# Recurrent outputs stored as split pairs, and the softmax factors, high parts and gather of an attention stage moved to other engines

## Chip, cores and metric

The kernel runs on one core of one Trainium2 chip. The metric is the device time of one execution in microseconds (us). Engines are called by the profile's short names: PE is TensorE (matmuls), DVE is VectorE, ACT is ScalarE, POOL is GpSimd, SP is SyncE, whose queue issues most of the DMAs.

## What is computed

One decoder block with two branches over a sequence of 2048 tokens and a width of 1024. One wide projection feeds a recurrence (causal convolution, then a gated linear scan) and an attention over three dilated windows. Each branch is multiplied by a gate and projected, the two are merged, projected again and normalised.

```python
proj = h @ w_in[l]
x_rnn, z_rnn, q, k, v, z_attn, g_r, g_a = jnp.split(proj, IN_SPLITS, axis=-1)
xc = causal_depthwise_conv(x_rnn, conv_w[l], conv_b[l])
hr = rg_lru(xc, w_a[l], b_a[l], w_x[l], b_x[l], lam[l], positions)
y_rnn = (hr * jax.nn.silu(z_rnn.astype(jnp.float32))).astype(dt) @ w_out_rnn[l]
...
o = dilated_attention_mixture(qh, kh, vh).reshape(B, S, D_ATTN)
y_attn = (o * jax.nn.silu(z_attn.astype(jnp.float32))).astype(dt) @ w_out_attn[l]
merged = jax.nn.sigmoid(g_r + bg_r) * y_rnn + jax.nn.sigmoid(g_a + bg_a) * y_attn
x = x + gate[:, None, :] * (merged @ w_o[l])
return rms_norm(x, g_final)
```

## The kernel before

**Split operands.** Every fp32 matmul operand is held as a rounded high part (type float32r) and a low part, the difference. A product is three matmuls (`mm3`, L147): high by high, high by low, low by high. `hi_act` (L152) rounds on ACT and `hi_dve` (L155) on DVE; `lo_pool` (L158) subtracts on POOL and `lo_dve` (L161) on DVE. The page books these under L153, L156, L159 and L162.

**First stage.** Two halves of the sequence (f = 0 and 1) run through the input projection by a Strassen scheme (`strassen`, L270; seven products of twelve matmuls each). In between, `recurrent` (L596) runs for eight channel blocks m. Its work on a half has ten steps spread over the products that follow (`steps_after`, L202): taps, gates, exponentials, scan, and at step 10 `finish` (L678), which multiplies the scan by the gate on DVE in the tile `zs` and stores 128x512 fp32 to the scratch tensor `yaT` on SP. The order in this stage comes from a scheduler with its own time model. `zs` has two buffers.

**Attention stage.** From L1361 on, the order is written by hand. 16 heads (8 for each half; the second half has more keys) have six units each: four of kind "c" (one class of token positions, both longer dilations) and two of kind "w" (the local blocks of 128). Time is cut into slots, one unit's scores to a slot. For a unit in slot s: PE makes the scores into PSUM (tag `sc`, two buffers), DVE takes the row minimum (`softmax_tile`, L983) and ACT the exponential with its sum into `st`. Seven slots later PE transposes the tile (`transposes_c`, `transposes_w`), `split_p` (L1057) splits it from PSUM into `pth` (high, ACT) and `ptl` (low, DVE), and a slot after that PE multiplies it by the values.

At the end of the slot ahead of the transposes, `scale` (L1046) multiplies the exponentials by a factor for each row, on DVE for "c" and on ACT for "w". Those factors are made once per head: `gather` (L1136, two POOL instructions, tile `sm`, at the tail of the head's last score slot), `exchange` in the next slot (one matmul into a third `sc` tile, so it needs one of the two buffers back from the row minimum), `maxima` on DVE, `exponentials` on ACT, `weights` on DVE. Within a slot the places are HEAD, scores, SOFTMAX, two thirds of the fill, EXCHANGE, one third of the fill, WEIGHTS, transposes, sums, TAIL.

**The fill.** `steps` (L1267) is a generator of matmul steps of the two output projections, some 3.2 to 3.6 steps (three 128x512 matmuls each) for each slot: four jobs on the recurrent outputs `yaT`, then two on the attention outputs `oT`. A job is 8 output blocks by 8 steps. While a job's last block (m = 7) runs, the operands `Y[j + 1, k]` of the next one are made: `load_y` (L1278) loads to `yraw` (four buffers) on SP, and `split_y` (L1285) makes `yh` on ACT and `yl` on POOL, eight buffers each, so that a buffer comes free when the step that reads it is done. Loads of keys, queries (`kraw`), values (`vraw`), weights (`w`) and gates (`fg`) go through the same SP queue in program order.

After the attention the rest of the fill runs, then the last products and the output projection with the final norm.

Of the kernel before, what the change touches and what calls it, by code (L numbers as in the profile page):

```python
# [20 lines left out]
P = 128  # L21
# [63 lines left out]
def decoder_block(ctx, tc, x, c, positions, g_norm, w_mod, b_mod, w_in, b_gate, conv_w, conv_b,  # L85
# [10 lines left out]
    def scratch(name, shape):  # L96
        return nc.dram_tensor(name, shape, F32, kind="Internal").ap()
# [54 lines left out]
    def hi_act(o, i):  # L152
        nc.scalar.activation(o, i, AF.Copy)  # L153
# [442 lines left out]
    def recurrent(rp, bigr, f, m):  # L596
# [25 lines left out]
        def x_part(j, ps, u):  # L622
# [67 lines left out]
        def done(i, j, ps, u):  # L690
            (z_part if i else x_part)(j, ps, u)
# [224 lines left out]
    def at(slot, place, fn, *args):  # L916
        plan.setdefault((slot, place), []).append((fn, args))
# [5 lines left out]
    class Head:  # L923
# [121 lines left out]

        def scale(self, kind, x):  # L1046
            for i, pp in enumerate(self.u[kind, x]):
                if kind == "c":
                    nc.vector.tensor_scalar(pp, pp, self.M[:, 0, x, i : i + 1], None, ALU.mult)  # L1049
                else:  # L1050
                    pp = pp[0][:, pp[1] :]
                    nc.scalar.activation(pp, pp, AF.Copy, scale=self.M[:, 1, i, x : x + 1])

        def transposes(self, kind, x):
            (self.transposes_c if kind == "c" else self.transposes_w)(x)

        def split_p(self, pt, cols):  # L1057
            th = T(ap_, [P, CH], F32R, "pth", bufs=4)
            tl = T(ap_, [P, CH], F32R, "ptl", bufs=4)
            hi_act(th[:, cols], pt[:, cols])  # L1060
            lo_dve(tl[:, cols], pt[:, cols], th[:, cols])
            return th, tl

        def transposes_c(self, r):
            pp, out = self.u.pop(("c", r)), []
            for k0 in range(0, self.bk[1] + 1, 2):
                pt = T(pT, [P, CH], F32, "pT")
                w = 2 * P + (P if k0 + 1 == self.bk[1] else 2 * P)
                for k in (k0, k0 + 1):
                    c0 = (k % 2) * 2 * P  # L1070
                    for j, i in enumerate([i for i, n in enumerate(self.bk) if n >= k]):
                        nc.tensor.transpose(pt[:, c0 + j * P : c0 + (j + 1) * P], pp[i][:, k * P : (k + 1) * P], ident)
                out.append(self.split_p(pt, slice(0, w)))
            self.u["tc", r] = out

        def transposes_w(self, i):

            pt_, out = self.u.pop(("w", i)), []
            for pieces in ((1, 2, 3, 4), (5, 6, 7, 0)):
                pt = T(pT, [P, CH], F32, "pT")  # L1080
                if self.bk[i] == 0 and 0 in pieces:
                    pieces = pieces[:3]
                for c, x in enumerate(pieces):
                    pp, half = pt_[x // 2][0], x % 2
                    nc.tensor.transpose(pt[:, c * P : (c + 1) * P], pp[:, half * P : (half + 1) * P], ident)
                out.append(self.split_p(pt, slice(0, len(pieces) * P)))
            self.u["tw", i] = out


# [46 lines left out]
        def gather(self):  # L1136

            self.sm = T(ap_, [P, 2, 4, 2, 8], F32, "sm")
            for g in range(2):
                nc.gpsimd.tensor_tensor(  # L1140
                    self.sm[:, g], self.st[:, :, g].rearrange("p t b n -> p t (b n)").unsqueeze(1).broadcast_to([P, 4, 2, 8]),
                    qm.unsqueeze(2).unsqueeze(3).broadcast_to([P, 4, 2, 8]), ALU.mult)

# [54 lines left out]
        def enlist(self, B):  # L1198
# [68 lines left out]
    def steps(jobs):  # L1267
# [8 lines left out]
                W[x] = load_wd(jobs[j][0], m, x % 2)  # L1276

        def load_y(j, k):  # L1278
            if j < len(jobs):
                w, ys, n = jobs[j]  # L1280
                assert ys is yaT or all((n // 2, h, n % 2) in stored for h in range(H))
                t = raw["y", j, k] = T(fl, [P, CH], F32, "yraw", bufs=4)
                nc.sync.dma_start(t[:], ys[k * P : (k + 1) * P, n * CH : (n + 1) * CH])
# [197 lines left out]
```

## Time and profile before

| | us |
|---|---|
| runs shown (median, lowest to highest) | 2396.06 (2392.12 to 2398.46) |
| the profiled execution, its own time | 2398.24 |
| its span, first to last instruction | 2396.5 |
| first attention scores to the last | 1508.7 to 2064.7 |
| loads of `yraw` from `yaT` | 1479.8 to 1754.6 |

In a row of the groups, the number after the bar is the busy time, then the mean of one instruction in ns; after the second bar stands the time for which the engine sat idle just ahead of these instructions and what ended it. In a timeline row the bracket holds the same for one instruction. In a row by stretches, each engine has its busy time and number of instructions; PEclk is the clock that PE was granted, as a share of full speed, and the next number is the busy share of the 16 DMA engines.

### The profile page before, as it was taken

What the parts mean: (1) busy time and instruction counts of PE and PEld (TensorE: products, weight loads), DVE (VectorE), ACT (ScalarE), POOL (GpSimd) and SP (SyncE); (2) the same over time, 40 slices, a digit from 0 to 9 for tenths busy, and PEclk for the clock granted to TensorE, in tenths of its full rate; (3) what the DMA queues carried; (4) which work ended last, traced back from release to release, by engine and by line L of the source; (5) the groups of instructions that cost most, each with busy time, mean ns of one, the idle gap of its engine ahead of it and who ended that gap; (6) DMA issues with size and microseconds to landing.
All of it is one profiled execution on the core that took longest, in us unless ns stands there. A gap on an engine that the chain in (4) does not pass through costs nothing.

```text
span 2396.5 us, 34064 instructions
## 1 busy us (share of the span) xinstructions
PE 2245.3 (94%) x11397; PEld 1884.5 (79%) x11397; DVE 1392.2 (58%) x2439; ACT 1137.7 (47%) x2268; POOL 1034.0 (43%) x813
## 2 busy tenths in 40 slices
PE   5899999999989999999999998999989898989998
PEld 5897777777777897878888876888878787878887
DVE  6847666766585734443444561477767787845433
ACT  3436656666542525555444411565666666522211
POOL 2566556665554643332211011456565757342000
PEclk9999999999999999999999998999999999999999
DMA  7266877677778559999666776988887678698752
GB/s 264 85 216 216 277 252 263 234 265 252 245 261 267 164 165 330 314 325 294 211 222 224 263 230 228 282 244 261 262 255 240 215 226 253 211 316 278 234 189 97
DMA packets 416295, 577.06 MB, mean 241 GB/s; under 512 B 71934, under 2 KB 278006, under 8 KB 415096
## 3 DMA queue, kind: packets, MB, share of 16 engines
q1 hardware_dynamic: 378680, 455.33, 60.7%
q10 hardware_dynamic: 37440, 119.55, 13.1%
q8 instruction: 90, 1.47, 0.2%
q14 instruction: 85, 0.70, 0.1%
HBM read 362.95 MB, written 211.82 MB: 240 GB/s over the span
## 4 chain that ended last, share of the span: by engine, by line
PE 55%; DMA 10%; DVE 10%; issue 9%; POOL 7%; ACT 5%; SPq 3%; ACTq 1%; POOLq 0%; DVEq 0%
PE pj L145 42%; PE pq L145 7%; PE pg L145 2%; PE sc L145 1%; PE o L145 1%; POOL S L159 1%; DMA wraw<-in_w_in_dram 1%; POOL yl L159 1%; DVE acc L485 1%; DMA wD<-s 1%; POOL vh L159 1%; POOL kq L159 1%; DMA yraw<-yaT 1%; DMA fg<-mrT 1%; DMA vraw<-vN 1%
## 5 line engine op out<-in xcount | busy, mean ns | idle before, releaser
L145 PE MATMUL pj<-T,S 128*128 128x512 f32 x4704 | 1121.5, 398 | 28.6 <-DVE ev L338 17.3
L145 PEld LDWEIGHTS pj<-T,S 128*128 128x128 f32 x4704 | 890.4, 190 | 248.0 <-DVE ev L338 22.5
L145 PE MATMUL pj<-yh,w 128*128 128x512 f32 x1024 | 373.8, 410 | 10.7 <-ACT yh L153 10.7
L159 POOL TENSOR_TENSOR S<-wraw,S 128x512 fp32r<-128x512 f32 x168 | 240.0, 1441 | 176.0 <-ACT S L186 105.0
L145 PEld LDWEIGHTS pj<-yh,w 128*128 128x128 f32 x1024 | 197.6, 193 | 47.8 <-ACT yh L153 11.8
L987 ACT ACTIVATE pp<-pp,st 128x256 f32<-128x256 f32 (+3 forms) x256 | 133.5, 523 | 171.0 <-DVE st L986 171.0
L145 PE MATMUL pj<-yl,w 128*128 128x512 f32 x512 | 205.3, 401 | 2.6 <-POOL yl L159 2.5
L145 PE MATMUL pj<-S,T 128*128 128x256 f32 x1152 | 161.1, 295 | 11.3 <-POOL S L159 7.9
L162 DVE TENSOR_TENSOR ptl<-pT,pth 128x384 fp32r<-128x384 f32 (+1 forms) x160 | 94.8, 626 | 124.6 <-ACT pth L153 124.4
L145 PEld LDWEIGHTS pj<-S,T 128*128 128x128 f32 x1152 | 150.8, 200 | 13.7 <-POOL S L159 9.4
L159 POOL TENSOR_TENSOR S<-s,S 128x512 fp32r<-128x512 f32 x84 | 114.4, 1362 | 91.5 <-ACT S L186 55.3
L159 POOL TENSOR_TENSOR yl<-yraw,yh 128x512 fp32r<-128x512 f32 x64 | 84.8, 1350 | 125.7 <-DMA yraw<-yaT 63.5
L640 DVE SCALAR_TENSOR_TENSOR xc<-xr,par,xc 128x512 f32<-128x512 f32 x96 | 83.5, 870 | 60.5 <-ACT xc L634 57.4
L1049 DVE TENSOR_SCALAR pp<-pp,M 128x128 f32<-128x128 f32 (+3 forms) x128 | 117.3, 956 | 0.0
L159 POOL TENSOR_TENSOR wh<-vraw,wh 128x640 fp32r<-128x640 f32 (+1 forms) x32 | 48.3, 1510 | 159.2 <-ACT wh L153 135.9
L292 DVE TENSOR_TENSOR u<-pj,u 128x512 f32<-128x512 f32 x56 | 38.4, 685 | 134.7 <-PE pj L145 79.5
L145 PEld LDWEIGHTS pj<-yl,w 128*128 128x128 f32 x512 | 99.1, 194 | 19.0 <-POOL yl L159 5.8
L986 DVE CUSTOM_DVE_ANT_0 pp<-sc,msk 128x256 f32<-128x256 f32 (+3 forms) x256 | 102.7, 444 | 16.1 <-PE sc L145 15.7
L159 POOL TENSOR_TENSOR kq<-kraw,kq 128x512 fp32r<-128x512 f32 (+1 forms) x64 | 102.1, 1607 | 13.8 <-ACT kq L153 13.8
L145 PE MATMUL pq<-oh,mh 128*128 128x512 f32 x256 | 98.6, 394 | 8.9 <-ACT mh L153 8.9
L620 POOL TENSOR_TENSOR zs<-zs,sg 128x512 f32<-128x512 f32 x32 | 46.0, 1437 | 133.1 <-ACT sg L616 132.5
L145 PE MATMUL pq<-ol,mh 128*128 128x512 f32 x256 | 100.7, 393 | 0.0
(287 smaller groups left out, 3996.1 us busy)
## 6 DMA issues: line engine op xcount, KB each, us to landing
sD<-S ACTq DMA_DIRECT2D x196, 512.0 KB, 3.4
S<-sD SPq DMA_DIRECT2D x196, 512.0 KB, 5.3
w<-wD SPq DMA_DIRECT2D x128, 512.0 KB, 5.7
wraw<-in_w_in_dram SPq DMA_DIRECT2D x136, 256.0 KB, 3.4
wD<-s ACTq DMA_DIRECT2D x64, 256.0 KB, 4.0
T<-in_w_mod_dram SPq DMA_DIRECT2D x8, 1024.0 KB, 9.6
vN<-ev SPq DMA_DIRECT2D x64, 128.0 KB, 2.3
zaT<-ev SPq DMA_DIRECT2D x32, 256.0 KB, 3.4
```

What stands on the lines that cost most here:

```text
L145: last_mm[0] = nc.tensor.matmul(o, lhsT=l, rhs=r, start=st, stop=sp, **kw).ins
L159: nc.gpsimd.tensor_tensor(o, i, h.bitcast(F32), ALU.subtract)
L162: nc.vector.tensor_tensor(o, i, h.bitcast(F32), ALU.subtract)
L292: nc.vector.tensor_tensor(u2[:], Z[:], u1[:], ALU.add)
L485: nc.vector.scalar_tensor_tensor(acc[:], t[:, k, :], ca[:, k : k + 1], acc[:], ALU.mult, ALU.add)
L620: (2, lambda: nc.gpsimd.tensor_tensor(z[:], z[:], sg[0][:], ALU.mult))))
L640: nc.vector.scalar_tensor_tensor(xc, xr[:, i : i + CH], cw(i), xc, ALU.mult, ALU.add)
L986: nc.vector.tensor_tensor_reduce(pdst, s_ps, mask, 1.0, 3e38, ALU.add, ALU.min, m_)
L987: nc.scalar.activation(pdst, pdst, AF.Exp, bias=m_, scale=-1.0, accum_out=l_)
L1049: nc.vector.tensor_scalar(pp, pp, self.M[:, 0, x, i : i + 1], None, ALU.mult)
```

## The change

Five edits:

1. The recurrence gets two more steps. `halves` (step 11) makes the high part `yh` of the gated output on ACT and the low part, in place in `zs`, on POOL. `store` (step 12) writes both to `yaT`, which becomes twice as large.
2. In the fill, a job on `yaT` has no `yraw`, no ACT and no POOL work: `split_y` issues two SP loads straight into the buffers `yh` and `yl`. For jobs on `oT`, the odd k take the low part on DVE.
3. `scale` runs on ACT for both kinds.
4. `split_p` takes the high part of the local blocks ("w") on DVE.
5. `gather` runs on DVE, at the HEAD of the slot whose EXCHANGE uses it.

```diff
-    yaT = scratch("yaT", [D, S])
+    yaT = scratch("yaT", [2, D, S])
...
                 nc.vector.tensor_tensor(z4, v["y"][:].rearrange("p (j r) -> p r j", r=4), z4, ALU.mult)
+
+            def halves():
+                hi_act(new("yh", F32R), zs[j][:])
+                lo_pool(zs[j][:].bitcast(F32R), zs[j][:], v["yh"][:])
+
+            def store():
                 c0 = f * HALF + j * CH
-                nc.sync.dma_start(yaT[m * P : (m + 1) * P, c0 : c0 + CH], zs[j][:])
+                nc.sync.dma_start(yaT[0, m * P : (m + 1) * P, c0 : c0 + CH], v["yh"][:].bitcast(F32))
+                nc.sync.dma_start(yaT[1, m * P : (m + 1) * P, c0 : c0 + CH], zs[j][:])
...
-                (8, root), (9, scan), (10, finish)))
+                (8, root), (9, scan), (10, finish), (11, halves), (12, store)))
...
         def scale(self, kind, x):
             for i, pp in enumerate(self.u[kind, x]):
-                if kind == "c":
-                    nc.vector.tensor_scalar(pp, pp, self.M[:, 0, x, i : i + 1], None, ALU.mult)
-                else:
+                if kind == "w":
                     pp = pp[0][:, pp[1] :]
-                    nc.scalar.activation(pp, pp, AF.Copy, scale=self.M[:, 1, i, x : x + 1])
+                w = self.M[:, 0, x, i : i + 1] if kind == "c" else self.M[:, 1, i, x : x + 1]
+                nc.scalar.activation(pp, pp, AF.Copy, scale=w)
...
-            hi_act(th[:, cols], pt[:, cols])
+            hi(th[:, cols], pt[:, cols])
             lo_dve(tl[:, cols], pt[:, cols], th[:, cols])
...
-                out.append(self.split_p(pt, slice(0, w)))
+                out.append(self.split_p(pt, slice(0, w), hi_act))
...
-                out.append(self.split_p(pt, slice(0, len(pieces) * P)))
+                out.append(self.split_p(pt, slice(0, len(pieces) * P), hi_dve))
...
-                nc.gpsimd.tensor_tensor(
+                nc.vector.tensor_tensor(
...
-            at(e - 1, TAIL, self.gather)
+            at(e, HEAD, self.gather)
...
         def split_y(j, k):
             if j < len(jobs):
-                t = raw.pop(("y", j, k))
-                yh = T(fl, [P, CH], F32R, "yh", bufs=NY)
-                yl = T(fl, [P, CH], F32R, "yl", bufs=NY)
-                hi_act(yh[:], t[:])
-                lo_pool(yl[:], t[:], yh[:])
-                Y[j, k] = yh, yl
+                Y[j, k] = [T(fl, [P, CH], F32R, tag, bufs=NY) for tag in ("yh", "yl")]
+                yh, yl = Y[j, k]
+                w, ys, n = jobs[j]
+                if ys is yaT:
+                    for l, y in enumerate((yh, yl)):
+                        nc.sync.dma_start(y[:].bitcast(F32), ys[l, k * P : (k + 1) * P, n * CH : (n + 1) * CH])
+                else:
+                    t = raw.pop(("y", j, k))
+                    hi_act(yh[:], t[:])
+                    (lo_dve if k % 2 else lo_pool)(yl[:], t[:], yh[:])
```

More of the change, by code (lines that the diff above doesn't have):

```diff
@@ L1047, in scale, with split_p @@
             for i, pp in enumerate(self.u[kind, x]):
-                if kind == "c":
-                    nc.vector.tensor_scalar(pp, pp, self.M[:, 0, x, i : i + 1], None, ALU.mult)
-                else:
+                if kind == "w":
                     pp = pp[0][:, pp[1] :]
-                    nc.scalar.activation(pp, pp, AF.Copy, scale=self.M[:, 1, i, x : x + 1])
+                w = self.M[:, 0, x, i : i + 1] if kind == "c" else self.M[:, 1, i, x : x + 1]
+                nc.scalar.activation(pp, pp, AF.Copy, scale=w)
         def transposes(self, kind, x):
             (self.transposes_c if kind == "c" else self.transposes_w)(x)
-        def split_p(self, pt, cols):
+        def split_p(self, pt, cols, hi):
             th = T(ap_, [P, CH], F32R, "pth", bufs=4)
             tl = T(ap_, [P, CH], F32R, "ptl", bufs=4)
-            hi_act(th[:, cols], pt[:, cols])
+            hi(th[:, cols], pt[:, cols])
             lo_dve(tl[:, cols], pt[:, cols], th[:, cols])
@@ L1278, in load_y @@
         def load_y(j, k):
-            if j < len(jobs):
+            if j < len(jobs) and jobs[j][1] is not yaT:
                 w, ys, n = jobs[j]
-                assert ys is yaT or all((n // 2, h, n % 2) in stored for h in range(H))
+                assert all((n // 2, h, n % 2) in stored for h in range(H))
                 t = raw["y", j, k] = T(fl, [P, CH], F32, "yraw", bufs=4)
```

## Prediction

> **What bounds the kernel now.** I read the page's first part, then the stretches, then PE's idle time in the attention stage.
>
> ```profile
> span 2396.5 us, 34064 instructions
> PE 2245.3 (94%) x11397; PEld 1884.5 (79%) x11397; DVE 1392.2 (58%) x2439; ACT 1137.7 (47%) x2268; POOL 1034.0 (43%) x813
> ...
> 200.00:680.00 480.00, 456.83 (x1907) 363.49 (x1907) 316.95 (x375) 294.85 (x486) 285.55 (x202) 0.98 0.76 258
> 1478.00:1505.00 27.00, 14.54 (x38) 9.29 (x39) 0.69 (x1) 6.65 (x11) 12.57 (x10) 0.68 0.79 265
> 1505.00:1835.00 330.00, 310.40 (x1913) 272.98 (x1912) 222.69 (x645) 207.86 (x604) 193.93 (x199) 0.98 0.85 256
> 1835.00:2080.00 245.00, 226.05 (x1398) 198.51 (x1397) 189.66 (x428) 154.94 (x392) 144.50 (x120) 0.97 0.75 229
> ```
>
> PE is busy for 94%; no matmul is added or removed, so the change can only win or lose PE's idle time and its clock. In the attention (last two rows) PE idles 330 - 310.4 = 19.6 us and 245 - 226.05 = 18.95 us, 38.5 together. What it waits for there, by groups over 1505 to 2080:
>
> ```profile
> L145 PE MATMUL sc<-sm,msk 128*128 128x128 f32 x32 | 7.9, 333 | 24.6 <-POOL sm L1140 14.0 <-DVE st L986 10.6
> L1072 PE MATMUL pT<-cs,pp 128*128 128x128 f32 x299 | 49.7, 292 | 10.3 <-DVE pp L1049 10.3
> L1085 PE MATMUL pT<-cs,pp 128*128 128x128 f32 x232 | 30.8, 273 | 2.5 <-ACT pp L1052 2.5
> ```
>
> That is 37.4 of the 38.5: the exchange matmul, and transposes that wait for factors on DVE or ACT. The largest single ones in PE's timeline, and the clock behind two of them:
>
> ```profile
> 1564.09 0.79 PE L145 MATMUL sc<-sm,msk 128*128 128x128 f32 x2 [5.52 <-POOL sm L1140]
> 1660.36 0.80 PE L145 MATMUL sc<-sm,msk 128*128 128x128 f32 x2 [3.75 <-POOL sm L1140]
> 1758.31 0.49 PE L145 MATMUL sc<-sm,msk 128*128 128x128 f32 x2 [4.36 <-POOL sm L1140]
> 1870.32 0.49 PE L145 MATMUL sc<-sm,msk 128*128 128x128 f32 x2 [3.73 <-DVE st L986]
> 1990.28 0.46 PE L145 MATMUL sc<-sm,msk 128*128 128x128 f32 x2 [1.93 <-DVE st L986]
> ...
> 1564.10:1567.90 3.80, 3.80 (x12) 3.11 (x13) 2.61 (x6) 0.23 (x2) 3.51 (x4) 0.50 1.08 299
> 1870.40:1874.20 3.80, 3.80 (x18) 3.34 (x19) 2.96 (x7) 2.26 (x7) 3.80 (x4) 0.67 0.51 155
> ```
>
> The granted clock is 0.50 for 3.8 us after the first stall (1.9 us of work lost) and 0.67 after the fourth (1.25 us).
>
> **Exchange in the first half (edits 2 and 5).** The first three stalls, 13.6 us, have one cause: at a change of job `sm` stands in POOL's queue behind the low parts of the next operands.
>
> ```profile
> 1556.37 3.76 POOL L159 TENSOR_TENSOR yl<-yraw,yh 128x512 fp32r<-128x512 f32 x3 [1.34 <-ACT yh L153]
> 1561.59 1.27 POOL L159 TENSOR_TENSOR yl<-yraw,yh 128x512 fp32r<-128x512 f32 x1 [1.46 <-DMA fg<-grT]
> 1563.49 0.55 POOL L1140 TENSOR_TENSOR sm<-st,cs 128x64 f32<-128x64 f32 x2
> ```
>
> The change takes both out of that queue. On DVE the gather stands at the slot's head; the exponential sums it needs are ready, since DVE's last work of the slot before, `ptl`, waits for a `pth` that ACT makes after them. These waits go to zero, with three cold spells: 13.6 + 3 x 1.7 = 18.7 us gained.
>
> **Exchange in the second half (edits 3 and 5).** 24.6 - 13.6 = 11.0 us remain, and there the matmul waits for its PSUM buffer. DVE's timeline ahead of the stall that ends at 1990.28:
>
> ```profile
> 1987.24 1.82 DVE L1049 TENSOR_SCALAR pp<-pp,M 128x384 f32<-128x384 f32 x2
> 1988.98 0.68 DVE L1131 TENSOR_TENSOR yw<-o,zt 128x512 f32<-128x512 f32 x1
> 1989.58 0.54 DVE L986 CUSTOM_DVE_ANT_0 pp<-sc,msk 128x384 f32<-128x384 f32 x1
> ```
>
> PE stood still from 1990.28 - 1.93 = 1988.35. Without the scaling, DVE at 1987.24 would do the gather (0.5 us, below), `yw` 0.68 and the minimum 0.54, ending at 1988.96: 0.6 us of wait stays instead of 1.93. Eight heads keep 4.8 of the 11.0; with the fourth stall's cold spell 7.5 us come back.
>
> **The factors (edit 3).** Rows for 1505 to 2080, the first five by groups, the rest with shapes apart:
>
> ```profile
> L1049 DVE TENSOR_SCALAR pp<-pp,M 128x128 f32<-128x128 f32 (+1 forms) x122 | 111.8, 956 | 0.0
> L1140 POOL TENSOR_TENSOR sm<-st,cs 128x64 f32<-128x64 f32 x32 | 10.7, 355 | 0.4 <-ACT pp L987 0.4
> L1153 DVE TENSOR_TENSOR xq<-sc,cs 128x64 f32<-128x64 f32 x32 | 5.7, 219 | 10.1 <-PE sc L145 9.7
> L153 ACT ACTIVATE yh<-yraw 128x512 fp32r<-128x512 f32 x40 | 24.0, 621 | 8.4 <-DMA yraw<-yaT 4.6 <-DMA yraw<-oT 3.3 <-PE o L145 0.5
> L159 POOL TENSOR_TENSOR yl<-yraw,yh 128x512 fp32r<-128x512 f32 x40 | 51.0, 1302 | 19.4 <-ACT yh L153 18.0 <-DMA fg<-grT 1.5
> ...
> L1049 DVE TENSOR_SCALAR pp<-pp,M 128x512 f32<-128x512 f32 x29 | 33.7, 1163 | 0.0
> L1049 DVE TENSOR_SCALAR pp<-pp,M 128x128 f32<-128x128 f32 x32 | 24.1, 752 | 0.0
> L987 ACT ACTIVATE pp<-pp,st 128x512 f32<-128x512 f32 x32 | 22.9, 714 | 0.0
> L1052 ACT ACTIVATE pp<-pp,M 128x256 f32<-128x256 f32 x116 | 49.5, 499 | 0.0
> L1052 ACT ACTIVATE pp<-pp,M 128x128 f32<-128x128 f32 x8 | 3.1, 390 | 0.0
> L153 ACT ACTIVATE pth<-pT 128x512 fp32r<-128x512 f32 x81 | 45.0, 583 | 5.4 <-PE pT L1072 4.3 <-PE pT L1085 1.1
> L162 DVE TENSOR_TENSOR ptl<-pT,pth 128x512 fp32r<-128x512 f32 x81 | 53.9, 688 | 88.6 <-ACT pth L153 88.4
> ```
>
> DVE loses 112 us of scaling. It gains 64 high parts of local blocks (32 units, two tiles): DVE's read of the same PSUM tile takes 0.69 us, so 44 us; 32 gather instructions between 0.18 (the `xq` mean of 0.219, less overlap) and 0.355 us, 6 to 11; and eight low parts for `oT`, bounded by the 0.69 just named and the scaling's 1.16, 5 to 9. Net -48 to -57 of its 412 us (222.7 + 189.7). ACT gains 128 scalings of 0.39 to 0.71 us (widths 128 to 512, about 0.55): 71 us. It loses 64 high parts, 37 us, and 32 `yh` of about 0.62, 20 us: +14 on 363 us (207.9 + 154.9), so 66% busy. POOL only loses here.
>
> A factor is issued at the end of one slot and used after the next slot's fill, some 4 us later. On DVE it stood behind `ptl`; ACT has idle time there. Of the 10.3 us behind L1049 I leave a quarter, and let the 2.5 behind L1052 grow to 4: 7.7 - 1.5 = 6.2 us gained. The two extra DVE instructions in a "w" slot lie in the 88.4 us that DVE now waits for `pth`; without that cover they cost 44 us of DVE, not of PE.
>
> The Trainium skill's page "ScalarE: Activation LUTs", section "Rules for kernel authors", speaks against this edit: multiplication belongs on VectorE, faster per element. The page "Advanced Engine Details and Errata", section "VectorE Performance Modes", has the exception: two-port VectorE instructions and GpSimd block each other. This trace sides with the second: 752 ns on DVE against 390 on ACT for 128 columns. By the first rule step three would bring nothing and the second half's waits would stay, 2384 us; by the rows the sum below.
>
> **Loads in pairs (edit 2).** Each job on `yaT` loads 16 x 256 KB instead of eight, and now all within the last eight steps, as a buffer comes free only when its step is done. Rows of SP's waits (1510 to 2080), of the DMA issues and of the slice at the first job change:
>
> ```profile
> SPq L1241 <- PE pj L145: 70.8, 34, 6.1
> SPq L1283 <- POOL yl L159: 39.4, 14, 8.3
> ...
> yraw<-yaT SPq DMA_DIRECT2D x32, 256.0 KB, 5.7
> ...
> 1545.00:1570.00 25.00, 19.48 (x120) 17.15 (x119) 15.28 (x36) 14.97 (x38) 18.65 (x19) 0.86 0.92 286
> ```
>
> SP already waits for PE before each load of weights (34 times), so a wait for PE at each pair is nothing new; behind it stand keys, values, gates and weights, which ACT, DVE and PE need two slots later or more. The 96 units' scores span 556 us (the table above), 5.8 us a slot; with 3.6 steps to a slot a step is 1.6 us, and a pair has eight steps, 13 us, to land; now a load takes 5.7. But 4.2 MB in 13 us is 323 GB/s on top of 256, and the slice shows 286 at 0.92 busy, 311 when full: 7.5 MB then need 24 us, so the last pair, issued at 11, lands near 24, just when it is needed. Keys and values behind it come some 10 us late, with two slots (11.6 us) to spare. Bounds: nothing, or 5 us of stall and 1.9 of cold clock at three job changes, 21 us. I take 4, nearer to nothing because the estimate ends just in time. At the attention's start (the stretch 1478 to 1505) the split's 0.62 and 1.3 us drop out of the first step, while eight pairs arrive at 265 GB/s, 2 us each: as late as now. I take 0, within 3 either way.
>
> **The recurrence (edit 1).** 32 more roundings of 0.62 us on ACT, 32 low parts on POOL of 1.3, 8 MB more to store and 32 more issues on SP. The second half has idle time on all three; in the first (stretch 200 to 680) PE already idles 23 us, with POOL at 59% and ACT at 61%, some of it behind these very engines:
>
> ```profile
> 208.03 0.74 PE L145 MATMUL pg<-xh,gh 128*128 128x512 f32 x2 [1.78 <-ACT xh L153]
> 210.22 0.80 PE L145 MATMUL pg<-xl,gh 128*128 128x512 f32 x1 [1.45 <-POOL xl L159]
> ```
>
> `zs` is also held two products longer, and the scheduler orders everything anew. 16 low parts add 21 us to POOL's 286. Bounds: -5 (a luckier order) to +23 (the idle time doubles); I take +3, idle growing with POOL's load.
>
> **Sum.** -18.7 - 7.5 - 6.2 + 4 + 0 + 3 = -25.4 us. The profiled execution (2398.24, its span 2396.5 and 1.7 around it) lies 2.2 above the median of the runs, so 2396.06 - 25.4, or 2370.
>
> **Rivals.**
> - *Waits that only change owner.* The exchange still lacks its PSUM buffer, and transposes wait for ACT instead of DVE (what the first of the two rules would do). For it: the releaser of 10.6 us is `st`, not `sm`. Against it: DVE's queue above. Only the 18.7 comes back, less 7: 2384.
> - *The burst of loads decides.* The 21 us instead of 4: 2387. For it: 0.92 busy already. Against it: the last pair is just in time.
> - *The first stage loses its 23 us.* 2390. For it: full engines there; against: the two engines have 40% free.
> - *ACT becomes last, slower than before.* ACT's row of a "w" slot holds four exponentials, four scalings, values and keys; now "c" factors stand before them. Its price is the 2.5 us row at L1085, once per head: 16 x 2.5 = 40 us, less the 4 already counted, 2406. From eleven such waits on, the gain is gone. For it: that wait exists. Against: ACT at 63%, and only one such wait now.
>
> **How the numbers follow.** Forecast 0.58 (its own range 2354 to 2383), owner 0.14, burst 0.13, first stage 0.05, ACT 0.10. No change means within 0.3%, 2389 to 2403, about what a measurement of this kernel can tell. Spread by these times, faster is 0.58 + 0.11 (owner) + 0.09 (burst) = 0.78; same 0.03 + 0.04 + 0.04 (first stage) = 0.11; slower 0.01 + 0.10 (ACT) = 0.11. The range takes in three rivals and leaves out ACT's: 2352 (the attention's full gain, 38.5 of idle time and 6.3 of clock) to 2396.
>
> **What would show it.** Right: no `sm` wait on PE above 1 us in the first half; PE idle in the attention under 12 us; DVE's scaling row gone, ACT near 66%; `yh<-yaT` landing under 10 us at job changes. Wrong: PE waiting for `DMA yh<-yaT` or `yl`, for `ACT pp` at L1072, or for kraw and vraw through ACT; more than 30 us idle in 200 to 680; a wait on `st` as long as now.

## Result and profile after

| | before | after |
|---|---|---|
| median of the runs, us | 2394.09 | 2410.8 (2410.12 to 2411.98) |
| ratio, with 95% interval | | 1.007 [1.005, 1.0089] |
| span of the profiled execution, us | 2396.5 | 2410.2 |
| first attention score on PE, us | 1508.7 | 1548.7 |
| last attention score, us | 2064.7 | 2079.4 |

The change makes the kernel slower by 0.7%, a little but clear of the noise, where 2370 was forecast (the runs of before beside it had 2394.09). The last two rows of the table, from PE's timeline, say where. The attention, from first to last score, takes 2079.4 - 1548.7 = 530.7 us instead of 556.0: 25.3 gained. The stage in front of it takes 40.0 us longer. What follows the last score takes 330.8 instead of 331.8. That is 40.0 - 25.3 - 1.0 = 13.7, the difference of the spans.

The page's first lines and two stretches of the changed kernel (columns as before: length, busy time and instructions of PE, weight loads, DVE, ACT, POOL, then granted clock, DMA share, GB/s):

```profile
span 2410.2 us, 34040 instructions
PE 2255.0 (94%) x11397; PEld 1884.1 (78%) x11397; DVE 1331.6 (55%) x2415; ACT 1172.7 (49%) x2332; POOL 1013.0 (42%) x773
...
200.00:680.00 480.00, 441.96 (x1806) 347.09 (x1805) 300.15 (x323) 288.47 (x473) 298.80 (x210) 0.96 0.73 248
1548.70:2079.40 530.70, 511.40 (x3201) 452.02 (x3200) 347.28 (x1025) 374.19 (x1012) 282.93 (x250) 0.99 0.89 270
```

In 200 to 680 PE idles 480 - 441.96 = 38.0 us, 14.9 more than before. Over the whole stage, from the start to the first score, before and after:

```profile
0.00:1508.70 1508.70, 1413.51 (x6747) 1168.19 (x6748) 837.39 (x1137) 710.11 (x1167) 641.88 (x465) 0.98 0.73 243
```

```profile
0.00:1548.70 1548.70, 1430.89 (x6748) 1171.94 (x6749) 837.92 (x1136) 721.74 (x1190) 672.97 (x488) 0.97 0.74 243
```

PE's idle time rises from 95.2 to 117.8 us, 22.6 more, and the same 6,747 matmuls take 17.4 us longer at a slightly lower clock. That is the 40.

What the engines wait for in 200 to 680 (engine, what it was about to run, what released it: us in total, times, longest):

```profile
DVE s L242 <- POOL S L160: 47.1, 17, 4.3
DVE s L241 <- DMA wraw<-in_w_in_dram: 38.8, 5, 8.3
ACT yh L154 <- DVE zs L681: 22.5, 16, 2.9
PE pj L146 <- DVE ev L339: 20.8, 11, 2.7
POOL zs L160 <- ACT yh L154: 16.5, 7, 3.0
PE pg L146 <- ACT xh L154: 8.4, 5, 3.8
```

The third and fifth rows are new: ACT stands still 16 times, once a block, until the product is done, and POOL until ACT has rounded it. PE's own two rows had 14.4 and 1.8 us before. The second row, DVE's wait for weights, had 21.4 before; it has 25.6 in the run below with one store (one_store) and 31.2 in the one with two stores and no split (no_split), and no run shows how the stores bring it about.

And PE's waits in the attention, 1548 to 2080:

```profile
PE pj L146 <- DMA yh<-yaT: 8.2, 5, 3.6
PE pj L146 <- DMA yl<-yaT: 4.0, 7, 1.2
PE pT L1092 <- DVE ptl L163: 2.9, 1, 2.9
PE sc L146 <- DVE sm L1147: 2.4, 1, 2.4
```

Of the 24.6 us for the exchange one wait of 2.4 is left (and one of 0.2), and of the 12.8 for factors 1.1; 12.2 us of waits for the new pairs have come in.

### The profile page after: what moved, and what is told of

It is laid out like the page before. It is cut to its first block, busy times and chain, and to the rows that moved or that the text cites. A ratio compares the mean times of both kernels' runs of the same rounds, so it can differ in the third digit from the quotient of the medians.

```text
span 2410.2 us, 34040 instructions
## 1 busy us (share of the span) xinstructions
PE 2255.0 (94%) x11397; PEld 1884.1 (78%) x11397; DVE 1331.6 (55%) x2415; ACT 1172.7 (49%) x2332; POOL 1013.0 (42%) x773
## 4 chain that ended last, share of the span: by engine, by line
PE 46%; DMA 12%; DVE 3%; POOL 2%; issue 2%; ACT 2%; SPq 2%; ACTq 0%; DVEq 0%; POOLq 0%
PE pj L146 29%; PE pq L146 7%; PE sc L146 4%; PE o L146 4%; DMA wD<-s 2%; DMA yl<-yaT 2%; PE pT L1079 1%; PE pT L1092 1%; DMA wraw<-in_w_in_dram 1%; DMA vraw<-vN 1%; DMA w<-wD 1%; DMA mrT<-fg 1%; PE pg L146 1%; DMA qT<-t 1%; POOL s L160 1%
## 5 line engine op out<-in xcount | busy, mean ns | idle before, releaser
L146 PE MATMUL pj<-T,S 128*128 128x512 f32 x4704 | 1135.9, 401 | 46.0 <-DVE ev L339 26.3
L146 PEld LDWEIGHTS pj<-S,T 128*128 128x128 f32 x1152 | 150.5, 200 | 12.2 <-POOL S L160 7.9
L1059 ACT ACTIVATE pp<-pp,M 128x256 f32<-128x256 f32 (+3 forms) x256 | 118.3, 526 | 9.1 <-DVE M L1183 9.1
L160 POOL TENSOR_TENSOR vh<-vraw,vh 128x256 fp32r<-128x256 f32 (+1 forms) x64 | 66.5, 1040 | 108.4 <-ACT vh L154 85.6
L146 PE MATMUL pq<-oh,ml 128*128 128x512 f32 x256 | 99.7, 391 | 0.0
```

Source lines behind the costliest of these rows:

```text
L146: last_mm[0] = nc.tensor.matmul(o, lhsT=l, rhs=r, start=st, stop=sp, **kw).ins
L160: nc.gpsimd.tensor_tensor(o, i, h.bitcast(F32), ALU.subtract)
L1059: nc.scalar.activation(pp, pp, AF.Copy, scale=w)
```

## Experiments

Three moments stand for progress through the first stage: when DVE starts the 17th and the 32nd of the 32 products `finish` (the first of the second half of the sequence, and the last), and the first attention score. All from the timelines, in us; an empty cell is left out. Ratios are to the kernel before, timed beside each, and come from all its runs; the moments are of one profiled execution, which lay 5 to 7 us above the median of the runs in one_store, extra_ap and dep_ap, and 6 to 8 below it in no_split and dep_st1.

| kernel | ratio [95%] | 17th block | 32nd block | first score | last score |
|---|---|---|---|---|---|
| before | 1 | 938.5 | 1349.7 | 1508.7 | 2064.7 |
| after | 1.0070 [1.0050, 1.0089] | 963.4 | 1380.2 | 1548.7 | 2079.4 |
| attn_only | 0.9855 [0.9829, 0.9881] | 938.5 | 1352.5 | 1507.8 | 2032.3 |
| store_only | 1.0168 [1.0144, 1.0192] | 963.6 | 1375.0 | 1542.1 | 2099.5 |
| one_store | 1.0002 [0.9986, 1.0018] | 955.5 | 1375.3 | 1534.4 | 2071.5 |
| no_split | 0.9956 [0.9940, 0.9972] | 942.0 | 1358.8 | 1520.2 | 2048.5 |
| zs4 | 1.0074 [1.0054, 1.0095] | 965.2 | 1380.1 | 1549.5 | |
| dve_split | 1.0062 [1.0041, 1.0083] | 957.4 | 1376.2 | 1545.3 | |
| behind2 | 1.0095 [1.0073, 1.0117] | 968.0 | 1386.6 | 1550.1 | |
| behind4 | 1.0109 [1.0086, 1.0131] | 972.0 | 1392.5 | 1557.5 | |
| extra_p | 0.9887 [0.9872, 0.9901] | 941.6 | 1356.1 | 1511.5 | |
| extra_ap | 0.9884 [0.9861, 0.9907] | 944.5 | 1358.3 | 1514.1 | |
| dep_ap | 0.9917 [0.9899, 0.9934] | 954.8 | 1368.5 | 1526.9 | |
| dep_st1 | 0.9944 [0.9924, 0.9963] | 955.1 | 1367.8 | 1523.8 | |
| late_ap | 0.9937 [0.9922, 0.9952] | 955.0 | 1370.5 | 1528.6 | |
| late_full | 1.0087 [1.0069, 1.0105] | 966.9 | 1385.5 | 1548.4 | |
| factors_only | 0.9904 [0.9889, 0.9919] | 941.4 | 1356.1 | 1516.2 | 2044.6 |
| gather_only | 1.0099 [1.0076, 1.0123] | 941.8 | 1352.7 | 1512.7 | 2090.1 |
| deep_attn | 0.9811 [0.9795, 0.9828] | 927.4 | 1333.8 | 1493.0 | |
| deep_after | 1.0012 [1.0000, 1.0025] | 958.5 | 1364.1 | 1532.7 | |

Four kernels with the first stage of before (before, attn_only, factors_only, gather_only) differ by 3.3 us at the 17th block and by 8.4 at the first score. Steps below that are not read from single rows.

**The two halves of the change, apart.** attn_only is the kernel before with edits 3 to 5 (and the odd low parts of all jobs on DVE); store_only is the changed kernel with those taken back.

> The kernel before with the attention's edits alone (factors on ACT, local high parts and gather on DVE, odd low parts of all fill operands on DVE); the recurrence and yaT as before. Theory S (the loss sits in the first stage, which the two new steps of the recurrence lengthen by 41 us, and the attention's edits are sound): the first attention scores start at 1508 to 1510 us as before, the attention is 20 to 33 us shorter than 556, and the time is 2362 to 2376. Rival (the attention gained only because pairs are loaded instead of split there): low parts still queue on POOL and ACT, the attention is within 10 us of 556, and the time is 2386 or more.

> The changed kernel with the attention's edits (factors, high parts, gather, odd low parts) taken back; the recurrence stores pairs and the fill loads pairs. Theory S: first attention scores at 1545 to 1552 us; the three exchange waits behind low parts in the first half are gone, the second half's stay: attention 535 to 552 us; time 2420 to 2435. Rival (pairs cost nothing by themselves, the loss comes from an interplay with the attention's edits): time 2390 to 2400.

Stretches from first to last score, in the kernel before, attn_only and store_only:

```profile
1508.70:2064.70 556.00, 518.64 (x3202) 456.37 (x3201) 398.86 (x1043) 354.25 (x977) 331.39 (x312) 0.98 0.80 245
```

```profile
1507.80:2032.30 524.50, 509.14 (x3201) 451.37 (x3200) 360.02 (x1037) 385.04 (x1036) 299.38 (x263) 0.99 0.86 261
```

```profile
1542.10:2099.50 557.40, 523.28 (x3202) 456.56 (x3202) 386.89 (x1044) 344.43 (x954) 302.54 (x288) 0.97 0.86 256
```

Edits 3 to 5 alone take 31.5 us off the attention: idle time falls from 37.4 to 15.4, and the same 3,200 matmuls take 9.5 us less. The pairs alone take off nothing (557.4, where 535 to 552 was expected). The cause that the prediction gave was right, the outcome not: in store_only PE's waits for `sm` are gone, but loads have taken their place.

```profile
PE sc L146 <- DVE st L994: 12.0, 6, 3.8
PE pj L146 <- DMA yh<-yaT: 9.6, 6, 3.7
...
PE pj L146 <- DMA yl<-yaT: 2.8, 6, 0.9
```

**Which part of the recurrence's edit costs.** one_store leaves out the second store, no_split the rounding and the subtraction.

```diff
 one_store
-                nc.sync.dma_start(yaT[1, m * P : (m + 1) * P, c0 : c0 + CH], zs[j][:])
 no_split
-                hi_act(new("yh", F32R), zs[j][:])
-                lo_pool(zs[j][:].bitcast(F32R), zs[j][:], v["yh"][:])
```

> The changed kernel without the store of the low parts (the fill loads the high parts twice, so the low parts are left out of the products); rounding on ACT and low parts on POOL stay. Theory W (the new ACT and POOL work in the recurrence delays what PE waits for): first attention scores still at 1540 us or later. Theory Q (the second store on SP and its traffic do it): scores at 1515 us or earlier and a time near 2375. Theory O (it is the order that the scheduler happened to make): anything between, without a relation to what was left out.

> The changed kernel with the rounding on ACT and the subtraction on POOL left out of the recurrence (the unrounded product is stored twice); two stores, their traffic and the two steps stay. Theory W: first attention scores back at 1508 to 1518 us and a time of 2370 to 2382. Theory Q: scores at 1540 us or later, time near 2410. Theory O: between the two.

Without the split the first score comes 1548.7 - 1520.2 = 28.5 us earlier, without the second store 14.3: together 42.8, about the 40 lost. Both first scores, 1534.4 and 1520.2, lie between the bounds of W and Q, where O had put them: the split is the larger part, but neither is all of it. By the traces PE's order differs from the changed kernel's too, in some 330 of 11,397 matmuls in one_store and some 40 in no_split, so these two shares are not free of the order.

Of the store's share 9.4 us lie behind the 32nd block (168.5 us to the first score in the changed kernel, 159.1 in one_store, 159.0 before). Two stores alone don't bring them: no_split has 161.4 there, and dve_split below, with split and two stores, 169.1. The largest stall there, in PE's timeline of the changed kernel, of one_store and of the kernel before:

```profile
1475.93 42.01 PE L146 MATMUL pj<-T,S 128*128 128x512 f32 x168 [4.90 <-DMA S<-sD]
```

```profile
1461.58 42.07 PE L146 MATMUL pj<-T,S 128*128 128x512 f32 x180 [1.65 <-DMA S<-sD]
```

```profile
1435.06 42.07 PE L145 MATMUL pj<-T,S 128*128 128x512 f32 x180 [0.67 <-DMA S<-sD]
```

An operand that the second half reads back comes late. It is not stuck behind the stores of the recurrence: the last of them is issued at 1383.4, and the load at 1472.04, behind stores of keys in SP's queue.

```profile
1467.94 4.00 SPq L798 DMA_DIRECT2D kT<-t  x6
1472.04 0.56 SPq L268 DMA_DIRECT2D S<-sD  x1
```

Why it is issued so late stays open. In the changed kernel the 40 us around that stall run at a lower clock too:

```profile
1460.00:1500.00 40.00, 34.06 (x133) 26.43 (x132) 8.21 (x12) 3.06 (x5) 0.63 (x1) 0.91 0.83 254
```

**What about the split costs: buffers, place, engine.** zs4 gives `zs` four buffers. dve_split puts both steps on DVE. behind2 and behind4 have four buffers and place the split two and four products later in the first half of the sequence, behind what stands ahead on each queue there.

```diff
 dve_split
-                hi_act(new("yh", F32R), zs[j][:])
-                lo_pool(zs[j][:].bitcast(F32R), zs[j][:], v["yh"][:])
+                hi_dve(new("yh", F32R), zs[j][:])
+                lo_dve(zs[j][:].bitcast(F32R), zs[j][:], v["yh"][:])
 behind2
+                with tc.issue_after(last(nc.scalar)):
                     hi_act(new("yh", F32R), zs[j][:])
+                with tc.issue_after(last(nc.gpsimd)):
                     lo_pool(zs[j][:].bitcast(F32R), zs[j][:], v["yh"][:])
...
-                (8, root), (9, scan), (10, finish), (11, halves), (12, store)))
+                (8, root), (9, scan), (10, finish), (11 + 2 * (1 - f), halves), (12 + 3 * (1 - f), store)))
```

> The changed kernel with four buffers for `zs` instead of two, nothing else. HOLD (the product waits for a `zs` that the split and the two stores hold longer): the first score comes some 10 to 20 us earlier than the 1548.7 us of the changed kernel, and the time falls to about 2393 to 2400. WAIT (instructions of the split that stand and wait at the head of ACT's, POOL's and SP's queues hold up what the projection needs) and WORK (the added busy time itself): within 4 us of the changed kernel, 2407 to 2415. ORDER (the scheduler's order in the first stage happens to be worse): since this edit moves a few instructions, anything up to 10 us either way.

> The changed kernel with the rounding and the subtraction of the recurrence both on VectorE, behind the product that makes their input, so that neither ACT nor POOL waits for anything new; the order on TensorE is that of the changed kernel but for a few neighbours. VectorE gets 32 x (0.6 to 0.7) x 2 = 38 to 45 us more, ACT 20 and POOL 42 less. WAIT: first score at 1520 to 1530 us, time about 2385 to 2395. WORK: VectorE is the engine with the least idle time of the three, so the first score stays at 1545 or later, 2405 to 2420. ORDER: since TensorE's order is kept, within 5 us of the changed kernel.

> The changed kernel with four buffers for `zs`, and in the first half of the sequence the rounding, the subtraction and the first store are placed two to three products later: each is issued only behind the last ScalarE, GpSimd or SyncE instruction that stands ahead of it in the program at that place. The work is the same. WAIT: ScalarE's and GpSimd's waits for the split (42 us in 200 to 780) fall by half or more, the first score comes 8 to 15 us earlier than in the same kernel with four buffers alone, time about 2395 to 2402. WORK: within 3 us of that kernel. ORDER: any sign.

> The same, four to five products later. WAIT: the waits of the split are gone, the first score at 1520 to 1530 us, time about 2385 to 2395; if only a late start counts, it is at least as early as with two to three products. WORK: within 3 us of the kernel with four buffers alone, whatever the lag. ORDER: any sign, with no relation between the lag and the time.

zs4: nothing comes back, so the longer hold of `zs` is not it. dve_split: nothing either (17th block 6 us earlier, first score 3). That is what WORK and ORDER had forecast, and not WAIT: without the split's waits on ACT and POOL about the same time is lost, with DVE carrying the whole split. behind2 and behind4 miss, and don't test what they should: in behind2 the wait at ACT only gets a second cause, the store that still reads the one buffer of the rounded part, and POOL waits longer.

```profile
POOL zs L160 <- ACT yh L154: 23.1, 9, 4.2
...
ACT yh L154 <- DMA yaT<-yh: 14.8, 6, 3.3
ACT yh L154 <- DVE zs L681: 14.7, 8, 2.9
```

**Work against dependence.** These start from attn_only, whose recurrence is that of before, and add the split of the first half's 16 blocks, unstored. extra_ap and extra_p run it on an operand that has long been ready; dep_ap on the finished product; dep_st1 stores the rounded part as well.

```diff
 extra_ap
+                s = B["B11"][0][:, 0, :].bitcast(F32)
+                with tc.issue_after(last(nc.scalar)):
+                    hi_act(new("yh", F32R), s)
+                with tc.issue_after(last(nc.gpsimd)):
+                    lo_pool(new("yl", F32R), s, s)
 dep_ap
+                hi_act(new("yh", F32R), zs[j][:])
+                lo_pool(new("yl", F32R), zs[j][:], v["yh"][:])
```

> The kernel before with edits 3 to 5 of the change (recurrence as before), plus, for each of the 16 blocks of the first half of the sequence, one more rounding of 128x512 on ScalarE and one more subtraction of 128x512 on GpSimd from an operand that has long been ready into tiles that nobody reads; nothing is stored, nobody waits for them, TensorE's order is the same but for 71 of 9,028 rows. Beside 2363.1 us without them, finish of the 17th block at 938.5. CHAIN (in the first half the sums on VectorE, the roundings on ScalarE and the subtractions on GpSimd that make the projection's operands run one after another through few buffers, so that time added to any of the three queues is paid nearly in full, 1.9 us a block): 17th block 18 to 28 us later, time about 2380 to 2392. WAIT (only the split's dependence on the product just finished hurts): within 4 us of 2363. ORDER (the scheduler's new order is what costs): within 4 us of 2363, since the order is kept.

> The same with the 16 subtractions on GpSimd alone (1.3 us each, 21 us in all); TensorE's, VectorE's and SyncE's order is the same in every row. CHAIN: 17th block 12 to 20 us later, time about 2375 to 2385. WAIT and ORDER: within 4 us of 2363.

> The kernel before with edits 3 to 5, plus, in the first half of the sequence, the change's rounding of the finished product on ScalarE and the subtraction on GpSimd, into tiles that nobody reads or stores; the recurrence's result is stored as before. TensorE's and VectorE's order is that of the kernel without it in every row. Beside 2363.1 us, and 17th block finished at 938.5, without the split; 2365.9 and 944.5 with the same work on an operand long ready. WAIT (the split's dependence on the product is what costs, as one link in the chain of queues): 17th block at 955 or later, time 2376 to 2390. ORDER or STORE (the order that the scheduler makes once a store hangs behind the split, or the store's place in SyncE's queue): 17th block at 940 to 948, time 2363 to 2370.

> The same plus one more store of 256 KB a block, of the rounded part, issued by SyncE behind ScalarE's rounding; TensorE's order differs in 916 lines. ORDER or STORE: 17th block at 952 or later, time 2375 to 2390. WAIT: no more than 4 us beside the kernel without the store.

The bare work, a rounding of 0.62 us and a subtraction of 1.21 in each of 16 blocks, moves the 17th block by 6.0 us, against the 18 to 28 that a chain paying each us in full would have cost. The same two instructions hung on the product move it by 10.3 us more (954.8, and 955.1 and 955.0 in two relatives of dep_ap), though in dep_ap the orders of PE, DVE, ACT and POOL, the added instructions aside, are those of attn_only in every row. So neither a new order nor the bare work is the main cost in this half; hanging the split on the product is. The times agree, less sharply: ratios of 0.9884 and 0.9887 for extra_ap and extra_p, 0.9917 to 0.9944 for dep_ap and its relatives. Two things came along with the dependence. In extra_ap the added rounding runs some 10 us or more before the product in 15 of the 16 blocks, and never waits, so the place in the queue changed too. And the subtraction takes 1.48 us in dep_ap instead of 1.21, 4.3 in all, so up to that much of the 10.3 may be work.

One more store, in dep_st1, adds nothing to the first stage of the profiled execution. Its median time is 8.2 us above that of dep_ap all the same, beyond the 4 that WAIT allowed, so what that store costs is not settled. The second one, which waits for POOL's subtraction, does: 955.5 in one_store, 963.4 in the changed kernel; two stores without the split (no_split) come to 942.0.

How it works can be followed at the eighth block. The timeline of extra_ap (start, length, what; in brackets the idle time before it and what ended it):

```profile
407.26 1.08 DVE L680 TENSOR_TENSOR zs<-y,zs 128x512 f32<-128x512 f32 x1
...
407.94 1.14 ACT L186 ACTIVATE S<-wraw 128x512 fp32r<-128x512 f32 x2
...
408.69 3.11 POOL L159 TENSOR_TENSOR S<-wraw,S 128x512 fp32r<-128x512 f32 x2 [2.55 <-ACT S L186]
...
413.93 0.69 DVE L241 TENSOR_TENSOR s<-s,wraw 128x512 f32<-128x512 f32 x1 [2.09 <-POOL S L159]
```

and of dep_ap:

```profile
413.65 1.07 DVE L680 TENSOR_TENSOR zs<-y,zs 128x512 f32<-128x512 f32 x1
...
414.75 0.63 ACT L153 ACTIVATE yh<-zs 128x512 fp32r<-128x512 f32 x1 [0.90 <-DVE zs L680]
...
415.53 1.67 POOL L159 TENSOR_TENSOR yl<-zs,yh 128x512 fp32r<-128x512 f32 x1 [2.99 <-ACT yh L153]
...
417.15 2.56 POOL L159 TENSOR_TENSOR S<-wraw,S 128x512 fp32r<-128x512 f32 x2
...
421.00 1.77 DVE L241 TENSOR_TENSOR s<-s,wraw 128x512 f32<-128x512 f32 x1 [3.76 <-POOL S L159]
```

In both, the two operands that PE needs next go ACT, POOL and then DVE's next sum. In extra_ap POOL starts on them 1.43 us after the product has begun. (The added pair had run 10 us earlier.) In dep_ap ACT first stands 0.90 us for the product, and POOL takes the product's low part first: it starts on the operands 3.50 us after, 2.1 later, and DVE's next sum is 0.7 us later (7.35 instead of 6.67). At the first half's last product dep_ap is 665.4 - 653.3 = 12.1 us behind extra_ap, 0.76 a block.

**Taking the wait away.** late_ap is dep_ap with the split two products later; late_full the changed kernel with that, three buffers for `zs` and two for the rounded part.

> The kernel before with edits 3 to 5 and the unstored split of the first half, as in the run that had it at its place (2377.6 us, 17th block at 954.8), but two products later, each issued behind the last ScalarE or GpSimd instruction that stands ahead of it there. TensorE's and VectorE's order is the same in every row in all three. WAIT: ScalarE's wait for the product (23.6 us in 200 to 680) falls to under 6, GpSimd's for the rounding (19.9) too, and the 17th block comes at 942 to 948, as with the same work on an operand long ready (944.5); time 2363 to 2370. If the dependence costs for another reason: 952 or later, 2374 to 2382.

> The changed kernel with three buffers for zs and two for the rounded part, and in the first half of the sequence rounding, subtraction and both stores two products later, behind what stands ahead of them there. Beside 2410.8 us and a 17th block at 963.4 in the changed kernel. WAIT: ScalarE's waits for product or store before the rounding fall under 8 us in 200 to 680 and the 17th block comes 8 to 16 us earlier, time about 2395 to 2404. If the waits only move to the stores in SyncE's queue or to zs: within 5 us of 2410.8.

Both miss, and again the condition was not met. In late_ap only the last of the 16 roundings and one subtraction stand elsewhere in the queues than in dep_ap, so it is nearly a second dep_ap, and the waits stayed (23.6 and 19.9 us in dep_ap):

```profile
ACT yh L153 <- DVE zs L680: 22.7, 15, 2.9
...
POOL yl L159 <- ACT yh L153: 16.8, 7, 3.0
```

In late_full ACT's wait for the product is 22.9 us. That the instructions stand at the head of their queues is thus seen in the rows, but a version in which they don't was not had.

**The attention's edits, apart.** factors_only is before with edit 3, gather_only before with edit 5.

```diff
 factors_only
-                    nc.vector.tensor_scalar(pp, pp, self.M[:, 0, x, i : i + 1], None, ALU.mult)
...
+                nc.scalar.activation(pp, pp, AF.Copy, scale=w)
 gather_only
-                nc.gpsimd.tensor_tensor(
+                nc.vector.tensor_tensor(
...
-            at(e - 1, TAIL, self.gather)
+            at(e, HEAD, self.gather)
```

> The kernel before with edit 3 alone: all factors scaled by ScalarE. The prediction's terms: 6.2 us of transposes' waits and, with VectorE free, most of 7.5 us of the second half's exchange: 2382 to 2390. If ScalarE becomes the last (the prediction's rival): above 2396. If VectorE's free time also brings the first half's waits down: below 2380.

> The kernel before with edit 5 alone: the gather of the exchange on VectorE at the head of the slot. The prediction's terms: the three sm waits of the first half and their cold clock go, 13 to 19 us, and nothing in the second half: 2377 to 2383. If the waits only change their owner (the exchange lacks its PSUM buffer): 2388 or more. If it does more than that term: below 2374.

Edit 3 alone takes 2044.6 - 1516.2 = 528.4 us for the attention, 27.6 less than before. The time, 2374.9, lies in the range of the expectation's last case, but not for its reason: PE's waits for row minima and nearly all of those for factors are gone, and the first half's waits for `sm` stay.

```profile
PE sc L145 <- POOL sm L1139: 17.1, 6, 5.4
PE pT L1084 <- ACT pp L1051: 1.7, 1, 1.7
PE pT L1071 <- ACT pp L1051: 1.2, 2, 1.0
```

Edit 5 alone takes 577.4, 21.4 more than before. In gather_only the gather stands in DVE's queue behind the scaling that edit 3 would have taken away:

```profile
1562.22 2.06 DVE L1049 TENSOR_SCALAR pp<-pp,M 128x128 f32<-128x128 f32 x2
1564.20 0.35 DVE L1140 TENSOR_TENSOR sm<-st,cs 128x64 f32<-128x64 f32 x2
...
1564.60 0.49 PE L145 MATMUL sc<-sm,msk 128*128 128x128 f32 x2 [2.01 <-DVE sm L1140]
```

and PE's waits for row minima, 10.6 us before, become the largest of the stage; the gather now stands ahead of them on the same engine. It is slow there too: the 26 of its 32 instructions that a POOL instruction overlaps take 0.76 us on average, the other six 0.22, as do 29 of 32 in the changed kernel.

```profile
PE sc L145 <- DVE st L986: 30.5, 8, 5.2
PE sc L145 <- DVE sm L1140: 9.2, 7, 3.3
```

**A version faster than both.** deep_attn and deep_after give the sums `s2` of the projection's left operands a second buffer.

```diff
-        s2 = T(wq, [P, KH, P], F32, "s2", bufs=1)
+        s2 = T(wq, [P, KH, P], F32, "s2", bufs=2)
...
-        nc.vector.tensor_tensor(s2[:], a12, s2[:], ALU.subtract)
+        s3 = T(wq, [P, KH, P], F32, "s2", bufs=2)
+        nc.vector.tensor_tensor(s3[:], a12, s2[:], ALU.subtract)
```

> The kernel before with edits 3 to 5, and two buffers instead of one for the sums `s2` of the projection's left operands, so that VectorE need not wait until GpSimd has split the last one. CHAIN: VectorE's waits for `S` (67 us in 200 to 680 in the kernel before) fall to a half or less and the first half is 5 to 15 us shorter, time about 2350 to 2358. WAIT: nothing to gain, 2360 to 2366. ORDER: up to 5 us either way.

> The changed kernel with the same two buffers. CHAIN: it gains more than the kernel before does, 10 to 25 us, since the split's time is then hidden behind the next sum: about 2386 to 2400, first score before 1538. WAIT: the split's waits stay, within 5 us of 2410.8. ORDER: up to 5 us either way.

The first score comes 14.8 us earlier in deep_attn and 16.0 in deep_after, and deep_attn at 2348.91 us is 1.9% faster than the kernel before. Time and first score of deep_after are those of CHAIN, but it does not gain clearly more than deep_attn, and the loss of the changed kernel stays: 1532.7 - 1493.0 = 39.7 us. The second buffer does not hide the split, so it is not that buffer through which the split delays the sums.

## Why the prediction was wrong

**The step that failed is "The recurrence (edit 1)": +3, with bounds -5 to +23; measured +40.0.** It priced the split by POOL's load and asked whether the engines had time left. Bare work is indeed cheap (6.0 us by the 17th block). It named no dependence, though each of the 32 blocks puts an instruction that waits for DVE's product into ACT's queue, one that waits for ACT into POOL's, and behind them stand the roundings and subtractions of the operands that PE needs next. The runs give 28.5 us for the split at the first score and 14.3 for the second store. By the 17th block the split comes to 16.3 in dep_ap, 6.0 as work and 10.3 from hanging it on the product, and the second store to 7.9; the second half's share was not taken apart, nor was the way by which the second store costs. The upper bound fell too: it doubled the 23 us of idle time of one stretch. That stretch gained 14.9 and the whole stage 22.6; what the bound left out is that the matmuls run slower as well, 17.4 us. (By its own terms the sum is 2370.7 and the lower end of the range 2351; nothing hangs on either.)

**The rival "the first stage loses its 23 us"** named the right place at too low a price and a chance of 0.05.

**The attention's sum held, its terms did not.** Predicted were -18.7 - 7.5 - 6.2 + 4 = -28.4, measured -25.3. That these are close is luck: edits 4 and 5 on top of edit 3 gave 3.9 (31.5 - 27.6) where 18.7 was priced, and edit 3 gave twice its 13.7.
- *Loads in pairs, +4 (0 to 21):* attn_only's 31.5 against the changed kernel's 25.3 makes 6.2, within the bounds.
- *Exchange in the first half, -18.7, edits 2 and 5:* the queue on POOL was the cause, as store_only shows, but neither edit brings the time: edit 2 puts 12.4 us of load waits in the place of the 14.0, edit 5 alone costs 21.4. On top of edit 3 it works: from factors_only to attn_only (edits 4 and 5 more, and the odd low parts on DVE) the waits for `sm` fall to 3.4 us, and the attention from 528.4 to 524.5.
- *Exchange in the second half and factors, -13.7, edit 3:* the size was off. Edit 3 alone gives 27.6. PE's idle time falls by 17.6 us in it, since no wait for a row minimum is left (4.8 us were to stay), and its matmuls take 10.0 less, which the prediction counted for the four largest stalls only. Factors of 128 columns on ACT took 0.396 us in factors_only, those on DVE 0.752 before:

```profile
L1051 ACT ACTIVATE pp<-pp,M 128x128 f32<-128x128 f32 x40 | 15.9, 396 | 6.3 <-DVE M L1175 6.3
```

The Trainium skill's page "ScalarE: Activation LUTs", section "Rules for kernel authors", puts multiplication on VectorE as the faster place, with its factor stated for bf16. For the fp32 factors of this kernel the measurement decides against it, but only beside a busy POOL. In the trace of before, the seven factors of 128x512 that no POOL instruction overlaps took 0.47 us each on DVE, the other 25 from 0.51 to 1.53, 1.27 on average; on ACT, in factors_only, they take 0.72 with or without POOL. One pair of factors (384 and 512 columns) beside POOL nearly throughout, and one during which POOL stops at 2042.32:

```profile
1967.58 1.27 POOL L1190 TENSOR_TENSOR zt<-zt,yw 128x512 f32<-128x512 f32 x1
1967.71 2.81 DVE L1049 TENSOR_SCALAR pp<-pp,M 128x384 f32<-128x384 f32 x2
1968.81 1.42 POOL L159 TENSOR_TENSOR vh<-vraw,vh 128x512 fp32r<-128x512 f32 x1
...
2041.02 1.30 POOL L1190 TENSOR_TENSOR zt<-y,yw 128x512 f32<-128x512 f32 x1
2042.08 0.85 DVE L1049 TENSOR_SCALAR pp<-pp,M 128x384 f32<-128x384 f32 x2
```

So the prediction chose rightly between its two rules.

**The other signs.** Two signs of being wrong came: 38.0 us idle in 200 to 680 (over 30), and PE waiting for `yh` and `yl`. One of being right failed: PE still waits 2.39 us for `sm` once in the first half, at 1638.6. ACT is 374.19 / 530.7 = 70.5% busy and did not become last (66% forecast); "ACT becomes last" and "waits that only change owner" did not happen. PE's idle time in the attention is 19.3 us, not under 12: the pairs' waits. The start of the attention, 0 within 3: PE's waits for operands over 0.3 us there are 8.29, 0.36, 1.16, 0.71 and 0.45 us, 11.0 in all, against 12.9 before.

**Open:** whether an order in which ACT and POOL don't stand for the product would bring the 10.3 us back. dve_split, with no such wait, loses about as much, which fits a split that delays DVE's queue instead, but no run shows that.

## What to carry to other kernels

Where several engines prepare the matmul's operands in turn, price an added step by what queues behind it on each engine and by what it waits for, not by idle shares: a rounding and a subtraction a block cost 0.4 us as free work and 1.0 when they waited for a product (6.0 and 16.3 us over 16 blocks). Measure edits of a bundle apart: here one half was worth 1.45% and the other cost 1.7%. An instruction moved to an engine goes behind that engine's queue, so a move that pays together with another (the gather, once the scaling is gone) can cost by itself.

## What was not expected of the hardware

PE's matmuls took more or less time over whole stages, and not only behind long stalls. The same 3,200 matmuls of the attention took 507 to 528 us, at granted clocks of 0.99 to 0.96. In four kernels idle and busy time moved together against before: -22.0 and -9.5 us (attn_only), -18.1 and -7.2 (after), -17.6 and -10.0 (factors_only), +11.7 and +9.7 (gather_only):

```profile
1516.20:2044.60 528.40, 508.66 (x3202) 451.90 (x3202) 306.21 (x926) 412.19 (x1094) 326.62 (x311) 0.98 0.85 258
```

```profile
1512.70:2090.10 577.40, 528.29 (x3202) 464.32 (x3201) 425.75 (x1073) 357.02 (x977) 323.84 (x282) 0.96 0.79 236
```

The first row is factors_only, the second gather_only. But two kernels don't follow. In store_only (0.97) idle time falls by 3.2 us and the matmuls take 4.6 more, and in one_store idle time falls by 18.3 and the matmuls take only 0.6 less:

```profile
1534.40:2071.50 537.10, 518.03 (x3201) 457.59 (x3200) 344.06 (x1025) 373.09 (x1011) 282.27 (x250) 0.97 0.89 266
```

So the matmuls' time goes with the granted clock, but idle time summed over a stage does not tell that clock. What sets it between 0.96 and 0.99 is not shown here, and a price in clock for each us of idle time can't be read from these runs.
